# From the first projection to attention in a decoder trunk: finishing the projection's sums one by one, and another order of modulation rows and scores

## The chip, the core and the metric

The kernel runs on one core of a Trainium2 chip, in float32 from end to end. The metric is the device time in microseconds (us) of one execution, as the median of several runs. A profile is a recording of one further execution. PE is TensorE's matmul, PEld its weight load, DVE is VectorE, ACT ScalarE, POOL GpSimd and SP SyncE, which here only issues transfers (DMA).

## What is computed

The reference is one layer of a conditioned decoder, with a sequence of 512 tokens, a model width of 1024 and a feed-forward width of 2816. Cut to what matters, with the names of the code:

```python
mod = silu(c) @ w_ada + b_ada                       # six modulation rows of 1024
shift1, scale1, gate1, shift2, scale2, gate2 = split(mod, 6)

h = rmsnorm(x, norm1_g) * (1 + scale1) + shift1
qa, ka, va, qd, kd, vd, ga, gd = split(h @ w_in)    # 512,128,128,512,512,512,1024,1024 columns
out_a = sliding_window_attention(qa, ka, va)        # 8 query heads, 2 key/value heads of 64,
                                                    # window 128, ALiBi, a sink for each head
out_d = diff_attention(qd, kd, vd, lam)             # 4 heads, softmax1 - lam * softmax2, causal,
                                                    # ALiBi, RMS norm of each head
merged = sigmoid(ga) * (out_a @ w_branch_swa) + sigmoid(gd) * (out_d @ w_branch_diff)
x = x + gate1 * (merged @ w_out)
h2 = rmsnorm(x, norm2_g) * (1 + scale2) + shift2
x = x + gate2 * conv_ffn(h2)                        # up, causal convolution of width 3, GELU * gate, down
return rmsnorm(x, final_g)
```

The four modulation rows `gate1` to `gate2` are needed only behind the attention stage; `shift1` and `scale1` are needed at the very start.

## The kernel before

**Arithmetic.** Each float32 operand of a matmul is split into a high part, rounded to the matmul's number format (`f32r`), and a low part, the rest. A product is three matmuls: high by high, high by low, low by high (`mm3`). ACT writes the high part and DVE the low part (`split` for weights, `evac` for results that are read out of PSUM). Activations lie transposed, with channels on the partitions.

**PSUM.** Its eight banks (128 x 512 float32 each) are given out by tags: two of `f` (projections), three of `s` (scores), two of `t` (transposes) and one of `v` (attention values). A tile that takes a bank waits until the last reader of the bank's previous tile is through.

**Raw weights.** All weights and also the pieces of `w_ada` land in tiles of the tag `raw`, of which there are four. A transfer into such a tile is issued by SP once the tile's former contents have been read.

**The start.** Two modulation vectors, the norm of x and its transposes are made, and the first projection goes along with them: columns 0 to 767 of `w_in`, which are four blocks of 128 columns of q (two heads each), one of k and one of v. Its six sums, `acc6`, lie in six banks: `a0` and `a1` in the `f` banks, `a2` to `a4` in the `s` banks, `a5` in the `v` bank. There are eight groups, one for each 128 rows of `w_in`, and in each group `mm_k` does 18 matmuls in three parts (high by high, low weights, low h), each part over all six sums. In this stage the order on DVE, ACT and PE is that of the text.

**Reading the sums.** `evac` then reads q blocks 0 to 3 (L430), k (L432) and v (a copy `vaT`, L434); v is turned by four PE transposes into the bank `pva` (L436 to L438) and read from it into `va` (L441), which POOL has zeroed (L435). One transpose of small convolution weights (`pcv`, L445) comes next in the text.

**The attention stage.** From here to the stage's end the order on PE is that of the text, and that on ACT, DVE and POOL is decided by a scheduler, which puts first what is marked with `high_priority`: the work of scores, softmax and transposes with an offset `HP`, the modulation rows with half of it. PE's order is a weave of two kinds of work:

- Attention steps. `swa_scores(i, n0)` does the scores of a pair of heads (i of 4) for two blocks of queries; DVE adds the mask and takes maxima (L547). `swa_softmax(i)` has DVE compute the shifts (`nm`, L558), ACT the exponentials and DVE the sums and the scaling (L570). `swa_transpose(i, j)` turns the probabilities into the banks `tp` (L582), two banks for each head, which `evac` reads into `pTh` and `pTl`. `swa_values(i)` multiplies by v. The difference attention has the same four steps, `diff_scores`, `diff_softmax` (L670 to L685, tiles `sd`, `dmx`, `dls`), `diff_transpose` (L693) and `diff_values`, over s = 0 to 15, that is four heads by four blocks of queries.
- Projection units, queued by `add_head(h)` (q, k and v of head h of the difference attention, into `pq`, `pk` and so on) and `add_gate_a(j)` (the gate and the branch projection of 128 columns). `fill(n)` gives n ticks of them, and a tick is one `mm3` of 128 x 512. The numbers of ticks between attention steps are `SWA_FILL` and `DIFF_FILL`:

```python
    fill(SWA_FILL[0])
    swa_scores(0, 0)
    fill(SWA_FILL[1])
    swa_scores(0, 2)
    swa_softmax(0)
    fill(SWA_FILL[2])
```

After this the loop over the four pairs interleaves scores and softmax of pair i + 1 with transposes and values of pair i, and behind the loop come the units that are left and the loop over s.

**Modulation rows.** `ada_rows` computes the four later rows in halves of 512 columns. Each step loads 256 rows of `w_ada` (`ra`, L741) and adds two products on DVE (`arow`, L746 and L748); four steps make a half row. `fill` calls one step at every tick that is divisible by `ADA_EVERY` (8), from tick `ADA_START` (4) on. Behind the fourth step of a half row the sums are split, and one tick later `ada_spread` adds them over the partitions with two matmuls (`pr`, L757 and L758), copies them (L760) and has POOL write them to `mod_rows` in DRAM (L761), from where they are read behind the attention stage.

**The rest.** The gates of the difference branch, the merge, `w_out`, the feed-forward part (most of its matmuls are in L1112) and the last norm are the same in both kernels.

Of the kernel before, what the change touches and what calls it, by code (L numbers as in the profile page):

```python
# [8 lines left out]
F32 = mybir.dt.float32  # L9
# [5 lines left out]
P = 128  # L15
D = 1024
S = 512
KT = D // P
NT = S // P
# [9 lines left out]
ST = 6  # L29
ADA_LAG = 1  # L30
ADA_EVERY = 8
ADA_START = 4
V_LAG = 13
STAT_LAG = 10
NORM_LAG = 16
SWA_FILL = (4, 2, 3, 2, 2, 2, 2, 3)
DIFF_FILL = (3, 2, 4, 2)
WARM = 14
GROUPS = ((0,), (1,), (2,), (3,), (4,), (5,), (6,), (7,))
# [13 lines left out]
def kernel(  # L53
# [22 lines left out]
    nc = tc.nc  # L76
# [15 lines left out]
    def fbank(name):  # L92
        return bank("f", 2, [P, S], name)

    def sbank(name, shape=(P, S)):
        return bank("s", 3, list(shape), name)

    def tbank(name, shape=(P, S)):
        return bank("t", 2, list(shape), name)

    def vbank(name):
        return bank("v", 1, [P, S], name)
# [25 lines left out]
    ident = cpool.tile([P, P], F32, name="ident")  # L128
# [66 lines left out]
    hTh, hTl = parts_of("h"), parts_of("l")  # L195
# [28 lines left out]
    )  # L224
    nc.sync.dma_start(crow[0:66, :], conv_w[0].rearrange("t (a p) -> (t a) p", p=P))
    nc.sync.dma_start(crow[66:88, :], conv_b[0].rearrange("(a p) -> a p", p=P))
    acc6 = [fbank("a0"), fbank("a1"), sbank("a2"), sbank("a3"), sbank("a4"), vbank("a5")]
    man = ExitStack()
    man.enter_context(tc.manual_schedule(engines={nc.vector.engine, nc.scalar.engine, nc.tensor.engine}))
    cs = cpool.tile([P, 8], F32, name="cs")  # L230
# [91 lines left out]

    def mm_k(k, part):
        wh, wl = wts[k]
        lhs, rhs = ((wh, hTh), (wl, hTh), (wh, hTl))[part]
        for i in range(6):
            nc.tensor.matmul(
                acc6[i], lhs[:, i * P : (i + 1) * P], rhs[k],
                start=k == 0 and part == 0, stop=k == KT - 1 and part == 2,
            )  # L330


    def keep_warm(n):
# [88 lines left out]
    def evac(hi, lo, src, scale=None):  # L422
        if scale is None:
            nc.scalar.copy(hi, src)
            nc.vector.tensor_sub(lo, src, hi.bitcast(F32))
        else:
            nc.scalar.activation(hi, src, AF.Copy, scale=scale)
            nc.vector.scalar_tensor_tensor(lo, src, scale, hi.bitcast(F32), ALU.mult, ALU.subtract)

    for i in range(4):  # L430
        evac(qa[:, i, 0], qa[:, i, 1], acc6[i], qsc[:, i : i + 1])
    evac(ka[:, 0], ka[:, 1], acc6[4])  # L432
    vT = ap.tile([P, S], F32, tag="tmp", bufs=2, name="vaT")
    nc.scalar.copy(vT, acc6[5])  # L434
    nc.gpsimd.memset(va.bitcast(F32), 0.0)  # L435
    pv = tbank("pva")  # L436
    for t in range(NT):
        nc.tensor.transpose(pv[:, t * P : (t + 1) * P], vT[:, t * P : (t + 1) * P], ident)  # L438
    pv3 = pv.rearrange("p (t d) -> p t d", t=NT)
    for a, cc in ((0, 0), (64, 192)):  # L440
        evac(va[:, 0, :, cc : cc + 64], va[:, 1, :, cc : cc + 64], pv3[:, :, a : a + 64])  # L441


    pcv = tbank("pcv", (P, 88))
# [37 lines left out]
    def fill(n):  # L482
        for _ in range(n):
            if not current:
                prefetch()
                if loaded:
                    wts, run = loaded.pop(0)
                    current.append(run(wts))
                    prefetch()
            if current:  # L490
                try:
                    next(current[0])
                except StopIteration:
                    current.clear()
            for e in list(later):
                e[0] -= 1
                if e[0] <= 0:
                    later.remove(e)
                    e[1]()
            tick[0] += 1  # L500
            if tick[0] >= ADA_START and tick[0] % ADA_EVERY == 0:
                next(ada, None)
# [17 lines left out]
    def swa_scores(i, n0):  # L520
        if n0 == 0:
            c = pairs[i] = Pair()
            c.mx, c.nm, c.lsum, c.es = (
                ap.tile([P, 2, NT], F32, tag=t, bufs=2, name=f"{t}{i}") for t in ("mx", "nm", "lsum", "es")
            )
            c.sb = [ap.tile([P, 2, P], F32, tag="st0", bufs=2, name=f"st{i}_0")]
            c.sb += [ap.tile([P, 2, 256], F32, tag="st", bufs=ST, name=f"st{i}_{n}") for n in range(1, NT)]
            c.pT = []
        c = pairs[i]
        sps = [sbank(f"sw{i}_{n0}_{j}", (P, 2, 256)) for j in range(2)]  # L530
        for n in (n0, n0 + 1):
            w = P if n == 0 else 2 * P
            k0 = max(0, n - 1) * P
            qs, ks = slice(n * P, (n + 1) * P), slice(k0, k0 + w)
            mm3_rows([
                (
                    sps[j][:, n - n0, :w],
                    [qa[64 * j : 64 * j + 64, i, b, qs] for b in range(2)],
                    [ka[64 * j : 64 * j + 64, b, ks] for b in range(2)],
                )  # L540
                for j in range(2)
            ])
        for n in (n0, n0 + 1):
            w = P if n == 0 else 2 * P
            for j in range(2):
                with tc.high_priority(offset=HP):
                    nc.vector.tensor_tensor_reduce(  # L547
                        c.sb[n][:, j, :w], sps[j][:, n - n0, :w], dsw[:, 256 - w : 256], 1.0, -3e38, ALU.add, ALU.max,
                        c.mx[:, j, n : n + 1],
                    )  # L550
# [119 lines left out]
    def diff_softmax(s):  # L670
        with tc.high_priority(offset=HP):
            h, n = divmod(s, NT)
            slope = 2.0 ** (-2 * (h + 1))
            mx, pm = scored[s]
            lsum = ap.tile([P, 2], F32, tag="dls", bufs=3, name=f"dls{h}_{n}")
            nc.vector.tensor_scalar_mul(mx, mx, -slope)  # L676
            for m in range(2):
                nc.scalar.activation(  # L678
                    pm[m], pm[m], AF.Exp, bias=mx[:, m : m + 1], scale=slope, accum_out=lsum[:, m : m + 1]
                )  # L680
            nc.vector.reciprocal(lsum, lsum)
            nc.vector.tensor_mul(lsum[:, 1:2], lsum[:, 1:2], nlam)
            nc.vector.tensor_scalar_mul(pm[1], pm[1], lsum[:, 1:2])
            nc.vector.scalar_tensor_tensor(pm[0], pm[0], lsum[:, 0:1], pm[1], ALU.mult, ALU.add)
            probs[s] = pm[0]  # L685
# [112 lines left out]
    fill(SWA_FILL[1])  # L798
    swa_scores(0, 2)
    swa_softmax(0)  # L800
    fill(SWA_FILL[2])
    for i in range(SWA_PAIRS):
        more = i + 1 < SWA_PAIRS
        if more:
            swa_scores(i + 1, 0)
        fill(SWA_FILL[3])
        swa_transpose(i, 0)
        fill(SWA_FILL[4])
        swa_transpose(i, 1)
        if more:  # L810
            swa_scores(i + 1, 2)
        fill(SWA_FILL[5])
        if more:
            swa_softmax(i + 1)
        fill(SWA_FILL[6])
        swa_values(i)
        fill(SWA_FILL[7])
# [4 lines left out]
    ta = big.tile([P, KT, S], F32, tag="qa", name="ta")  # L822
    for j in range(2):
        add_gate_a(j)
    diff_scores(0, 1)
    diff_softmax(0)
    diff_softmax(1)
    fill(DIFF_FILL[0])
    for s in range(4 * DIFF_HEADS):
        h, n = divmod(s, NT)  # L830
# [412 lines left out]
    last = range(KT - TAIL, KT)  # L1243
# [482 lines left out]
```

## Time and profile before

| what | value |
|---|---|
| three runs, us | 719.83, 719.99, 721.53 |
| median, us | 719.99 |
| profiled execution, us | 722.67, with a span of 720.9 |
| mean granted clock of TensorE | 0.988 of full speed |
| PE busy | 693.5 us (96% of the span) |
| PEld busy | 604.8 us (84%) |
| DVE busy | 589.0 us (82%) |
| ACT busy | 381.5 us (53%) |
| POOL busy | 84.7 us (12%) |
| HBM read, written | 121.85 MB, 2.11 MB |

The span goes from the first to the last recorded instruction; the profiled execution's own time is 1.8 us longer than its span. A row of the instruction view gives the start (us from the span's start), the busy time of the row's instructions together, the engine, line, operation, output and inputs, the shape and the count; in brackets stand the idle time ahead of it and what ended that. The parts that the change touches lie between 57 and 160 us of the span.

### The profile page before, as it was taken

The numbers are of one execution on the slowest core, as the hardware profiler recorded it, in microseconds if no ns is written. First come the engines' busy times: TensorE is split into PE (matmuls) and PEld (weight loads), VectorE is DVE, ScalarE is ACT, GpSimd is POOL, SyncE is SP. The second block draws the span as 40 slices with busy tenths as digits, with TensorE's granted clock in tenths as the row PEclk, the third lists the DMA queues.
The fourth block names the chain that finished last, engine by engine and source line by source line (L and its number), as shares of the span: only waits on it lengthen the run. The fifth ranks groups of instructions, "written<-read, shape, count | busy, mean of one in ns | idle before, by whom it ended". The sixth has DMA issues, their size and how long they took to land. (4 is left out here: it accounts for less than half of the span.)

```text
span 720.9 us, 11252 instructions
## 1 busy us (share of the span) xinstructions
PE 693.5 (96%) x4172; PEld 604.8 (84%) x4172; DVE 589.0 (82%) x1121; ACT 381.5 (53%) x673; POOL 84.7 (12%) x101
## 2 busy tenths in 40 slices
PE   5998899999999999999999999999999999999994
PEld 5776788877887888888889999999999999778883
DVE  5998777887986674875379899888888999889996
ACT  3644656454554233432358666555656666555662
POOL 4000000000100110000012021111111212640000
PEclk8999999999999999999999999999999999999998
DMA  9886222534634565726827698877879769998502
GB/s 303 287 265 195 71 59 61 175 101 133 176 109 155 181 196 179 234 88 210 248 68 147 152 198 206 200 175 212 198 202 217 162 174 253 206 206 220 181 0 118
DMA packets 117367, 124.70 MB, mean 173 GB/s; under 512 B 4511, under 2 KB 93376, under 8 KB 117312
## 3 DMA queue, kind: packets, MB, share of 16 engines
q1 hardware_dynamic: 98254, 97.71, 42.8%
q0 software_dynamic: 18720, 25.73, 20.9%
q8 instruction: 33, 0.54, 0.3%
q10 hardware_dynamic: 338, 0.54, 0.2%
q14 instruction: 22, 0.18, 0.1%
HBM read 121.85 MB, written 2.11 MB: 172 GB/s over the span
## 5 line engine op out<-in xcount | busy, mean ns | idle before, releaser
L1112 PE MATMUL up<-t,m_whi 128*128 128x256 f32 x528 | 96.1, 283 | 0.0
L1112 PEld LDWEIGHTS up<-t,m_whi 128*128 128x128 f32 x528 | 82.4, 192 | 0.0
L1112 PE MATMUL up<-t,m_wlo 128*128 128x256 f32 x264 | 74.7, 283 | 0.1
L1112 PE MATMUL up<-bh,p_wlo 128*128 128x256 f32 x232 | 65.7, 284 | 0.6 <-DVE p_wlo L1055 0.6
L1112 PE MATMUL up<-bh,p_whi 128*128 128x256 f32 x232 | 65.6, 283 | 0.0
L1112 PE MATMUL up<-bl,p_whi 128*128 128x256 f32 x232 | 65.6, 283 | 0.0
L1112 PEld LDWEIGHTS up<-t,m_wlo 128*128 128x128 f32 x264 | 50.6, 192 | 0.3 <-DVE m_wlo L1055 0.3
L1112 PEld LDWEIGHTS up<-bh,p_wlo 128*128 128x128 f32 x232 | 44.4, 192 | 1.1 <-DVE p_wlo L1055 1.1
L748 DVE SCALAR_TENSOR_TENSOR arow<-ra,cs,arow 128x512 f32<-128x512 f32 x56 | 41.9, 748 | 3.9 <-DMA ra<-in_w_ada_dram 3.3
L1112 PEld LDWEIGHTS up<-bh,p_whi 128*128 128x128 f32 x232 | 44.5, 192 | 0.0
L1112 PEld LDWEIGHTS up<-bl,p_whi 128*128 128x128 f32 x232 | 44.5, 192 | 0.0
L1023 POOL DMA_DIRECT2D s<-in_w_up_dram x21 | 27.2, 1385 | 143.2 <-DMA s<-in_w_up_dram 60.1
L1055 DVE TENSOR_TENSOR m_wlo<-s,m_whi 128x1024 fp32r<-128x1024 f32 x31 | 37.8, 1219 | 2.0 <-ACT m_whi L1051 2.0
L1051 ACT CAST m_whi<-s 128x1024 fp32r<-128x1024 f32 x31 | 32.4, 1047 | 9.4 <-DVE s L1045 6.0
L174 POOL TENSOR_TENSOR r<-ms,mhalf 128x1 f32<-128x1 f32 (+1 forms) x16 | 13.5, 844 | 172.9 <-DVE ms L172 106.0
L1112 PE MATMUL up<-t,p_whi 128*128 128x256 f32 x176 | 32.2, 283 | 0.0
L678 ACT ACTIVATE sd<-sd,dmx 128x128 f32<-128x128 f32 (+3 forms) x32 | 17.8, 556 | 22.1 <-DVE dmx L676 15.6
L761 POOL DMA_DIRECT2D mod_rows<-arow x8 | 4.3, 540 | 205.4 <-ACT arow L760 205.2
L1112 PEld LDWEIGHTS up<-t,p_whi 128*128 128x128 f32 x176 | 27.4, 192 | 0.2 <-issue 0.2
L1119 ACT ACTIVATE gT<-a,cv 128x512 f32<-128x512 f32 x22 | 17.7, 814 | 17.7 <-DVE a L1154 17.3
L1051 ACT CAST p_whi<-wa 128x1024 fp32r<-128x1024 f32 x18 | 18.7, 1041 | 12.1 <-PE up L1112 9.0
L1112 PE MATMUL up<-t,p_wlo 128*128 128x256 f32 x88 | 24.9, 283 | 0.0
(476 smaller groups left out, 2125.3 us busy)
## 6 DMA issues: line engine op xcount, KB each, us to landing
ra<-in_w_ada_dram SPq DMA_DIRECT2D x32, 512.0 KB, 4.2
wa<-in_w_up_dram SPq DMA_DIRECT2D x22, 512.0 KB, 4.3
s<-in_w_up_dram SPq DMA_DIRECT2D x21, 512.0 KB, 4.8
s<-in_w_up_dram POOLq DMA_DIRECT2D x21, 512.0 KB, 6.5
adaw<-in_w_ada_dram SPq DMA_DIRECT2D x16, 512.0 KB, 5.1
w<-in_w_in_dram SPq DMA_DIRECT2D x12, 512.0 KB, 4.6
a<-in_w_up_dram SPq DMA_DIRECT2D x11, 512.0 KB, 4.7
b<-in_w_down_dram SPq DMA_DIRECT2D x10, 512.0 KB, 4.3
```

The source lines that it names most:

```text
L174: nc.gpsimd.tensor_tensor(r0, ms, mhalf[:, :n], ALU.pow)
L678: nc.scalar.activation(pm[m], pm[m], AF.Exp, bias=mx[:, m : m + 1], scale=slope, accum_out=lsum[:, m : m + 1])
L748: nc.vector.scalar_tensor_tensor(ac, r[:, a], cc, ac, ALU.mult, ALU.add)
L761: nc.gpsimd.dma_start(mod_rows[idx : idx + 1, hf * S : (hf + 1) * S], row)
L1023: nc.gpsimd.dma_start(dst, upblock(*blk), accum_op=ALU.add)
L1051: nc.scalar.copy(W[J, name][0], R[J, SRC[name]])
L1055: nc.vector.tensor_sub(lo, R[J, SRC[name]], hi.bitcast(F32))
L1112: nc.tensor.matmul(o[u], w[:, k, cu], b[:, k], start=name in ("p1", "m5", "p2") and k == 0 and x == 0, stop=k == 3 and x == 2, skip_group_ ...
L1119: nc.scalar.activation(grow(j), av[J][:, u], AF.Identity, bias=cv[:, 66 + j : 67 + j], scale=cv[:, 44 + j : 45 + j])
```

## The change

Four things change, all between the first projection's last group and the first blocks of the difference attention:

- **The order of the sums.** The six sums are taken in the order `DONE` = 0, 4, 2, 5, 1, 3 (q0, k, q2, v, q1, q3), in the giving out of banks and in all matmuls. In the last group the two low parts of a sum follow one another, so the sums are finished one by one and not all in the last part. The sums are read in the order q0, k, q2, v, q1, q3.
- **The turn of v.** The four transposes of v and their reading stand in `turn_va`, which is called one tick after the first softmax.
- **Modulation rows and fills.** `ADA_START` goes from 4 to 12, so the first step runs at tick 16 and not at tick 8, and all steps are one multiple of 8 ticks later. The first three fills go from 4, 2, 3 to 2, 1, 6 (nine ticks in both).
- **Difference scores.** `diff_scores` and `diff_softmax` of the first two blocks move from behind the pair loop into its last turn, where the scores and the softmax of a next pair would stand.

```diff
@@ -29,11 +29,11 @@
 ST = 6
 ADA_LAG = 1
 ADA_EVERY = 8
-ADA_START = 4
+ADA_START = 12
 V_LAG = 13
 STAT_LAG = 10
 NORM_LAG = 16
-SWA_FILL = (4, 2, 3, 2, 2, 2, 2, 3)
+SWA_FILL = (2, 1, 6, 2, 2, 2, 2, 3)
 DIFF_FILL = (3, 2, 4, 2)
 WARM = 14
 GROUPS = ((0,), (1,), (2,), (3,), (4,), (5,), (6,), (7,))
@@ -224,7 +224,9 @@
     )
     nc.sync.dma_start(crow[0:66, :], conv_w[0].rearrange("t (a p) -> (t a) p", p=P))
     nc.sync.dma_start(crow[66:88, :], conv_b[0].rearrange("(a p) -> a p", p=P))
-    acc6 = [fbank("a0"), fbank("a1"), sbank("a2"), sbank("a3"), sbank("a4"), vbank("a5")]
+
+    DONE = (0, 4, 2, 5, 1, 3)
+    acc6 = {i: (fbank, sbank, vbank)[(0, 0, 1, 1, 1, 2)[i]](f"a{i}") for i in DONE}
     man = ExitStack()
     man.enter_context(tc.manual_schedule(engines={nc.vector.engine, nc.scalar.engine, nc.tensor.engine}))
     cs = cpool.tile([P, 8], F32, name="cs")
@@ -322,12 +324,15 @@
 
     def mm_k(k, part):
         wh, wl = wts[k]
-        lhs, rhs = ((wh, hTh), (wl, hTh), (wh, hTl))[part]
-        for i in range(6):
-            nc.tensor.matmul(
-                acc6[i], lhs[:, i * P : (i + 1) * P], rhs[k],
-                start=k == 0 and part == 0, stop=k == KT - 1 and part == 2,
-            )
+        last = k == KT - 1
+        if last and part == 2:
+            return
+        for i in DONE:
+            for p in (1, 2) if last and part else (part,):
+                lhs, rhs = ((wh, hTh), (wl, hTh), (wh, hTl))[p]
+                nc.tensor.matmul(
+                    acc6[i], lhs[:, i * P : (i + 1) * P], rhs[k], start=k == 0 and p == 0, stop=last and p == 2
+                )
 
 
     def keep_warm(n):
@@ -427,18 +432,26 @@
             nc.scalar.activation(hi, src, AF.Copy, scale=scale)
             nc.vector.scalar_tensor_tensor(lo, src, scale, hi.bitcast(F32), ALU.mult, ALU.subtract)
 
-    for i in range(4):
+    nc.gpsimd.memset(va.bitcast(F32), 0.0)
+
+    def evac_q(i):
         evac(qa[:, i, 0], qa[:, i, 1], acc6[i], qsc[:, i : i + 1])
+
+    evac_q(0)
     evac(ka[:, 0], ka[:, 1], acc6[4])
+    evac_q(2)
     vT = ap.tile([P, S], F32, tag="tmp", bufs=2, name="vaT")
     nc.scalar.copy(vT, acc6[5])
-    nc.gpsimd.memset(va.bitcast(F32), 0.0)
-    pv = tbank("pva")
-    for t in range(NT):
-        nc.tensor.transpose(pv[:, t * P : (t + 1) * P], vT[:, t * P : (t + 1) * P], ident)
-    pv3 = pv.rearrange("p (t d) -> p t d", t=NT)
-    for a, cc in ((0, 0), (64, 192)):
-        evac(va[:, 0, :, cc : cc + 64], va[:, 1, :, cc : cc + 64], pv3[:, :, a : a + 64])
+    evac_q(1)
+    evac_q(3)
+
+    def turn_va():
+        pv = tbank("pva")
+        for t in range(NT):
+            nc.tensor.transpose(pv[:, t * P : (t + 1) * P], vT[:, t * P : (t + 1) * P], ident)
+        pv3 = pv.rearrange("p (t d) -> p t d", t=NT)
+        for a, cc in ((0, 0), (64, 192)):
+            evac(va[:, 0, :, cc : cc + 64], va[:, 1, :, cc : cc + 64], pv3[:, :, a : a + 64])
 
 
     pcv = tbank("pcv", (P, 88))
@@ -798,20 +811,29 @@
     fill(SWA_FILL[1])
     swa_scores(0, 2)
     swa_softmax(0)
-    fill(SWA_FILL[2])
+    fill(1)
+    turn_va()
+    fill(SWA_FILL[2] - 1)
     for i in range(SWA_PAIRS):
         more = i + 1 < SWA_PAIRS
         if more:
             swa_scores(i + 1, 0)
+        else:
+            diff_scores(0)
         fill(SWA_FILL[3])
         swa_transpose(i, 0)
         fill(SWA_FILL[4])
         swa_transpose(i, 1)
         if more:
             swa_scores(i + 1, 2)
+        else:
+            diff_scores(1)
+            diff_softmax(0)
         fill(SWA_FILL[5])
         if more:
             swa_softmax(i + 1)
+        else:
+            diff_softmax(1)
         fill(SWA_FILL[6])
         swa_values(i)
         fill(SWA_FILL[7])
@@ -822,9 +844,6 @@
     ta = big.tile([P, KT, S], F32, tag="qa", name="ta")
     for j in range(2):
         add_gate_a(j)
-    diff_scores(0, 1)
-    diff_softmax(0)
-    diff_softmax(1)
     fill(DIFF_FILL[0])
     for s in range(4 * DIFF_HEADS):
         h, n = divmod(s, NT)
```

## The prediction

> **What bounds the kernel now.** I read the page first, then the granted clock and busy time in short windows, then the instructions of PE, DVE and SP from 57 to 100 us and from 118 to 160 us, the two places that the change touches.
>
> ```profile
> span 720.9 us, 11252 instructions
> PE 693.5 (96%) x4172; PEld 604.8 (84%) x4172; DVE 589.0 (82%) x1121; ACT 381.5 (53%) x673; POOL 84.7 (12%) x101
> 65.29:68.70 3.41, 1.53 (x13) 1.00 (x12) 3.41 (x7) 0.00 (x0) 0.00 (x0) 1.00 0.45 151
> 68.70:72.11 3.41, 3.41 (x14) 2.23 (x12) 2.53 (x12) 0.37 (x1) 0.00 (x0) 0.50 0.72 205
> 85.76:120.00 34.24, 34.24 (x231) 28.95 (x230) 25.10 (x93) 23.26 (x73) 0.00 (x0) 1.00 0.17 48
> 150.00:160.00 10.00, 8.88 (x54) 6.99 (x52) 9.87 (x31) 4.53 (x12) 0.25 (x1) 1.00 0.50 150
> ```
>
> The window rows give PE, PEld, DVE, ACT and POOL busy, the granted clock, the DMA share and GB/s. PE is busy 96% of the span: time can come only from PE's waits and from its clock. Just after the first projection DVE is full while PE works 1.53 of 3.41 us, and in the next 3.41 us the clock is halved. From 85.76 to 120 PE never stops, so what is won before it is kept unless a later wait takes it back. The waits themselves, on PE:
>
> ```profile
> 59.88 1.56 PE L327 MATMUL a<-hTlB,w0h 128*128 128x512 f32 x6
> 61.90 0.50 PE L118 MATMUL pq<-hThA,w_h 128*128 128x512 f32 x1 [0.46 <-DVE qa L428]
> 66.11 0.32 PE L125 MATMUL sw<-ka,qa 64*128 64x128 f32 x1 [0.61 <-DVE qa L428]
> 67.43 0.32 PE L125 MATMUL sw<-ka,qa 64*128 64x128 f32 x1 [1.00 <-DVE qa L428]
> 78.58 1.13 PE L582 MATMUL tp<-ident,st 128*128 128x128 f32 x7 [0.97 <-DVE st L570]
> 82.31 1.01 PE L582 MATMUL tp<-ident,st 128*128 128x128 f32 x7 [1.20 <-DVE pTl L425]
> 96.55 0.93 PE L582 MATMUL tp<-ident,st 128*128 128x128 f32 x7
> 157.97 0.30 PE L693 MATMUL td<-ident,sd 128*128 128x128 f32 x1 [1.12 <-DVE sd L684]
> ```
>
> Every releaser is DVE. These are its rows there, with the products of the modulation rows (arow) in 60 to 69 us as one group (DVE's busy time comes first), and the landing time of their loads:
>
> ```profile
> 61.10 0.75 DVE L428 SCALAR_TENSOR_TENSOR qa<-a,qsc,qa 128x512 fp32r<-128x512 f32 x1
> 64.64 0.75 DVE L748 SCALAR_TENSOR_TENSOR arow<-ra,cs,arow 128x512 f32<-128x512 f32 x1 [1.48 <-DMA ra<-in_w_ada_dram]
> 67.30 0.68 DVE L425 TENSOR_TENSOR ka<-a,ka 128x512 fp32r<-128x512 f32 x1
> 60.00:69.00 9.00, 3.58 (x6) 0.00 (x0) 0.00 (x0) 0.98 0.78 250
> DMA to landing us min/median/max: 3.7/4.2/5.1
> 59.55 0.37 SPq L741 DMA_DIRECT2D ra<-in_w_ada_dram  x1
> ```
>
> Between the low parts of the four q sums and of k (61.10 to 67.30) DVE does products and waits 1.48 us for a load issued at 59.55. The scores need k, so they wait for all of it.
>
> **Part 1, sums one by one, products later, other fills.** The number of matmuls is unchanged. In the last group the first sum's last matmul is the eighth of 18 instead of the thirteenth: five places of 1.56/6.7 = 0.23 us earlier. ACT reads it at about 59.2, DVE at 60.0. With k second in line and no product ahead, DVE has q0, k and q2 done at 60.0 + 0.66 + 0.6 + 0.66 = 61.9. The bank that pq waits for is free at 60.7, before PE's last sum, so its 0.46 us goes. The transpose for cv (0.24 us) moves ahead of the last group; that and the memset of va, on an idle POOL, cost nothing.
>
> The built order of the changed kernel shows what comes instead. DVE's queue becomes: q1 and q3 between two products of load 1, the split of v's weights, four score maxima, a product of load 2, and only then the other four maxima and the softmax; then the second product, the scaling, a product of load 3, and the reading of the first transposes. Load 2 uses load 1's slot and load 3 load 2's, so each is issued when DVE has done both products of the one before. A DMA latency thus stands in DVE's queue, with PE's scores and transposes behind it. On SP the loads move behind the next head's weights, which aren't needed before 95 us.
>
> I walk that queue with row durations (pitches: product 0.66, 512-wide low part 0.6 to 0.66, split 1.14, wide maximum 0.34; a duration in a row contains about 0.1 of overlap).
>
> ```profile
> 74.28 0.36 DVE L558 TENSOR_SCALAR nm<-mx,nsink 128x4 f32<-128x4 f32 x2
> 88.93 1.08 DVE L570 TENSOR_SCALAR st<-st,lsum 128x128 f32<-128x128 f32 x4
> 92.58 1.22 DVE L115 TENSOR_TENSOR w_l<-w,w_h 128x1024 fp32r<-128x1024 f32 x1
> 83.62 1.16 DVE L425 TENSOR_TENSOR pTl<-tp,pTh 128x512 fp32r<-128x512 f32 x2 [0.30 <-ACT pTh L424]
> 72.89 0.42 DVE L547 CUSTOM_DVE_ANT_0 st<-sw,dsw 128x256 f32<-128x256 f32 x1 [1.66 <-PE sw L125]
> ```
>
> Load 1 lands at 57.7 + 4.2 = 61.9, in time. Product, q1, product: 63.7, and load 2 goes out. q3, split, four maxima: 66.6. Load 2, with less traffic, takes 3.9 (between minimum and median) and lands at 67.65. Product, four maxima, nm: 69.95. Second product: 70.6; load 3 (alone: 3.7) lands at 74.4, while exponentials and the first scaling end at 73.6. Product to 75.05; then sums, va, second scaling (0.98) and three maxima, 2.75 us: 77.8. The first reading of transposes takes 0.6, and PE's second transposes start at 78.4 instead of 82.31: 3.9 earlier.
>
> DVE then has a backlog. Reading, product, q, reading, maxima, nm: 82.9. Load 4, issued at 79.5, lands at 83.2. From there two products 1.3, two splits 2.3, sums 0.4, two scalings 1.95 with 0.35 between, three 512-wide reads 1.8, four maxima 1.1: 9.25 us to 92.5, and 0.6 for the reading that frees the bank of PE's next second transposes: 93.1. PE could be there at 96.55 - 3.9 = 92.65. They start at 93.15: **3.4 us earlier** than before. After it DVE has no product until the last pair's values, so this stands. The ends: with every load at the 5.1 maximum the same walk gives 97.85, a loss of 1.3; with no load wait at all the gain is bounded by the waits in the PE rows and half of the slow clock window, 0.46 + 0.61 + 1.00 + 0.97 + 1.20 + 1.7 = 5.9. I take 3.4, since DMA is idle around loads 3 and 4.
>
> **Part 2, scores of the difference attention inside the last pair.**
>
> ```profile
> 122.25 0.68 DVE L425 TENSOR_TENSOR qkv<-pk,qkv 128x512 fp32r<-128x512 f32 x1
> 124.02 1.16 DVE L425 TENSOR_TENSOR pTl<-tp,pTh 128x512 fp32r<-128x512 f32 x2 [1.09 <-ACT pTh L424]
> 124.86 0.93 PE L582 MATMUL tp<-ident,st 128*128 128x128 f32 x7
> 134.02 0.41 ACT L678 ACTIVATE sd<-sd,dmx 128x128 f32<-128x128 f32 x1 [3.45 <-DVE dmx L676]
> 134.94 0.17 DVE L681 RECIPROCAL dls<-dls 128x2 f32<-128x2 f32 x1 [0.22 <-ACT sd L678]
> 135.65 0.35 DVE L684 SCALAR_TENSOR_TENSOR sd<-sd,dls,sd 128x128 f32<-128x128 f32 x1
> ```
>
> Before, PE meets no wait here: the last transposes start at 124.86, and the fills after them cover the softmax. Afterwards DVE's order puts the whole softmax of block 0 between the k read (ends 122.85) and pTl. Two maxima and a multiply: 123.4. ACT's two exponentials, ahead of its copy pTh, from 123.55 to 124.35. Reciprocal to last product, 134.94 to 135.92 in the rows: 125.35. First half of pTl 0.6: 126.0. PE arrives at 125.0 (two matmuls moved away, 0.46 less, six score matmuls more), waits 1.05, and 0.2 again for the second half. With 0.15 for a second short block of scores that is **1.4 lost**. Ends: 0, if ACT and DVE run ahead of PE by that much; 2.0, if the weights of the gate (split 0.6 before PE needs them) also come late.
>
> **Part 3, the wait at 157.97.** It stands behind four products:
>
> ```profile
> 150.00:158.00 8.00, 2.71 (x4) 0.00 (x0) 0.25 (x1) 1.00 0.43 130
> ```
>
> The new order has none there (these rows come later by 8 steps); a split of 1.14 and a read of 0.6 take part of their place. With both chains moved on by part 2 I get the result at 158.35 against PE at 158.25: of 1.12 about 0.25 stays, **0.85 won** (ends 0 and 1.1).
>
> The last modulation row comes 8 steps, some 6 us, later:
>
> ```profile
> 307.49 0.48 POOL L761 DMA_DIRECT2D mod_rows<-arow  x1 [21.72 <-ACT arow L760]
> 335.91 1.37 POOL L1023 DMA_DIRECT2D s_t<-in_w_up_dram  x1 [27.94 <-DVE c L936]
> ```
>
> POOL has 27.94 us free behind it: no cost. If that cover were gone it would cost those 6 us.
>
> **The sum.** -3.4 + 1.4 - 0.85 = -2.85. The profiled execution took 722.67 us at a span of 720.9, so 719.8; the median of the three runs is 719.99, which these waits belong to as well: 717.1. Ends for this case, from landing times of 3.7 to 4.2 us each and part 2 between 1.0 and 1.6: 715.9 to 718.4. 0.3% of the time, 2.2 us, is about what a measurement of this kernel can tell from no change; the threshold is at 717.8.
>
> **Rivals.**
> 1. The loads land late. For: 1.48 waited at 64.64 for a load of 5.1. Against: that was with DMA share 0.98 to 1, and the loads now go out when it is low. At 5.1 us each part 1 is +1.3: 719.99 + 1.3 + 1.4 - 0.85 = 721.8, slower. Part 1 falls by 4.7 for 1.2 us of mean landing time, so the sum is zero at 3.9 + 2.85/3.9 = 4.6 us.
> 2. The clock halves on the critical path. For: the first two window rows: a window with PE busy 1.53 of 3.41 and no wait over 1.00 us was followed by 3.41 us at 0.50. In the walk PE has nothing from 76.2 to 78.4, 2.2 us, more than the 1.88 idle there. Half speed for 3.41 us loses 1.7, less the 0.5 that PE waits for DVE anyway: 718.3. Against: the wait may fall across two such windows, and an earlier halving would be hidden in it. The Trainium skill (TensorE: Matmul & The Clock Gate, "HAM oscillation — how this bites in real kernels") asks only that no idle gap exceed some 3.4 us; by that this rival has no chance and the time stays 717.1. The trace disagrees: gaps of at most 1.00 us sufficed, so the rival keeps its chance.
> 3. Part 2 is free, because DVE reaches it ahead of PE: 717.1 - 1.4 = 715.7. Against: the k read and the copy of the pair's values come from PE itself.
> 4. It doesn't do what it says: DVE, full in both places, only trades one queue for another: 720.0.
>
> **Chances.** Forecast 0.50 (three quarters of it under 717.8), late loads 0.16, clock 0.13, free part 2 0.13, nothing won 0.08. Faster by over 0.3%: 0.38 + 0.13 + 0.01 = 0.52. Slower by over 0.3% needs late loads together with the clock or the 2.0 end: 0.10. Within: 0.38. The range leaves out a tenth on each side: 715.2 to 721.2.
>
> **What would show it.** Right: pq without a wait near 61.3; DVE waiting for ra loads before the second maxima (about 1 us) and before the product after the first scaling (about 0.8); second transposes near 78.4 and 93; a new wait of about 1 us on pTl in the last pair; the wait at 157.97 mostly gone. Wrong: no DVE wait on a load (part 1 nearer 5), waits of 2 us and more (rival 1), 0.50 clock after 78 us (rival 2), no wait in the last pair (rival 3).

## The result and the profile after

The changed kernel takes **730.19 us** (median of four runs, 729.82 to 730.97) beside 719.91 for the kernel before (four runs, 718.76 to 721.53): a ratio of **1.0134, 95% interval 1.0113 to 1.0155**. It is slower by 10.3 us, where 2.9 faster was forecast.

The head of the page after:

```profile
span 729.2 us, 11250 instructions
PE 695.7 (95%) x4172; PEld 605.5 (83%) x4172; DVE 588.6 (81%) x1121; ACT 381.2 (52%) x673; POOL 84.8 (12%) x101
```

PE is busy 2.2 us longer than before (695.7 against 693.5) and idle 6.1 us longer (33.5 against 27.4), so most of the loss is waiting. The changed kernel's lines have other numbers: L697 is the old L684 (the last product of a difference softmax), L761 the old L748 (a product for the modulation rows), L430 the old L425. PE's instructions after that carry the steps of the prediction (start, busy time, operation, and in brackets the idle time ahead and its releaser):

```profile
60.41 0.40 PE L118 MATMUL pq<-hThA,w_h 128*128 128x512 f32 x1
66.10 1.65 PE L125 MATMUL sw<-ka,qa 64*128 64x256 f32 x11 [1.52 <-DVE mx L560]
79.27 0.93 PE L595 MATMUL tp<-ident,st 128*128 128x128 f32 x7
93.83 1.01 PE L595 MATMUL tp<-ident,st 128*128 128x128 f32 x7 [0.22 <-DVE pTl L430]
123.58 1.01 PE L595 MATMUL tp<-ident,st 128*128 128x128 f32 x7 [1.00 <-DVE pTl L430]
153.08 0.63 PE L706 MATMUL td<-ident,sd 128*128 128x128 f32 x4 [0.99 <-DVE sd L697]
159.38 0.30 PE L706 MATMUL td<-ident,sd 128*128 128x128 f32 x1 [1.07 <-DVE sd L697]
204.13 0.63 PE L706 MATMUL td<-ident,sd 128*128 128x128 f32 x4 [0.78 <-DVE sd L697]
230.17 0.63 PE L706 MATMUL td<-ident,sd 128*128 128x128 f32 x4 [2.14 <-DVE sd L697]
314.63 0.50 PE L118 MATMUL pB<-outdA,wbd 128*128 128x512 f32 x1 [1.62 <-ACT wbd L114]
317.01 0.50 PE L120 MATMUL pB<-outdA,wbd 128*128 128x512 f32 x1 [1.64 <-DVE wbd L115]
341.32 0.50 PE L1187 MATMUL oc<-wo_h,mg0h 128*128 128x512 f32 x1 [0.68 <-DVE c L951]
```

Up to 94 us the second transposes of pairs 0 and 1 start earlier than before (79.27 and 93.83 against 82.31 and 96.55), and the one wait of the last pair, pair 3, is there. What the prediction did not have begins at 153: waits on `sd`, the softmax in the blocks of the difference attention, on `wbd`, weights of the difference branch, at 315, and on `c` at 341, the reading of a bank that the next sum (`oc`) takes over.

To see where the time goes, the table follows the same PE instruction in both kernels. The last matmul group that both have ahead of the first projection's last group is the reduction `pa`, before and then after:

```profile
55.17 0.58 PE L264 MATMUL pa<-ones,ac 128*128 128x1 f32 x4
54.21 0.58 PE L266 MATMUL pa<-ones,ac 128*128 128x1 f32 x4
```

The kernel after stands 0.96 us earlier there already. In that stretch the change alters only the order of the sums, and the 0.96 belongs to these executions: the profile before has two windows of 3.41 us at half the clock there (14.09 to 20.91), the one after has one (14.53 to 17.95), and two runs below have it the other way round: run 4, with the changed kernel's code up to there, has two and reaches `pa` at 55.07, and run 2, with the code of the kernel before, has one and reaches it at 53.69. So all differences are counted from this group on (start after - start before + 0.96; minus is a lead). The pairs are counted from 0, the difference blocks (four to a head) too.

| up to | lead or lag, us | gained or lost on the way |
|---|---|---|
| second transposes of pair 2, 110.8 us | -1.69 | -1.69 |
| second transposes of pair 3, 124.86 | -0.32 | +1.37 |
| difference block 4, 157.97 | +2.37 | +2.69 |
| block 7, 177.90 | +1.35 | -1.02 |
| block 15, 226.52 | +4.61 | +3.26 |
| first `oc`, 331.88 | +8.30 | +3.69 |
| end of the span | +9.26 | +0.96 |

The front gains, the last pair costs, and then 9.6 us are lost between 125 us and the end. Not all of a row is waiting, because some of PE's work stands on the other side of a mark in the changed kernel. PE's idle time in the table's rows from that of pair 3 on is, before and after, 0 and 1.00, 1.12 and 2.73, 0.37 and 0, 0.33 and 2.92, 0.46 and 3.50, 12.70 and 13.45 us.

### The profile page after: what moved, and what is told of

It is laid out like the page before. It is cut to its first block, busy times and chain, and to the rows that moved or that the text cites. A ratio compares the mean times of both kernels' runs of the same rounds, so it can differ in the third digit from the quotient of the medians.

```text
span 729.2 us, 11250 instructions
## 1 busy us (share of the span) xinstructions
PE 695.7 (95%) x4172; PEld 605.5 (83%) x4172; DVE 588.6 (81%) x1121; ACT 381.2 (52%) x673; POOL 84.8 (12%) x101
## 5 line engine op out<-in xcount | busy, mean ns | idle before, releaser
L761 DVE SCALAR_TENSOR_TENSOR arow<-ra,cs,arow 128x512 f32<-128x512 f32 x56 | 41.9, 749 | 3.8 <-DMA ra<-in_w_ada_dram 2.7
L1131 PEld LDWEIGHTS up<-t,p_whi 128*128 128x128 f32 x176 | 27.4, 192 | 0.2 <-issue 0.2
```

Of the source, the lines that this page charges most:

```text
L761: nc.vector.scalar_tensor_tensor(ac, r[:, a], cc, ac, ALU.mult, ALU.add)
L1131: nc.tensor.matmul(o[u], w[:, k, cu], b[:, k], start=name in ("p1", "m5", "p2") and k == 0 and x == 0, stop=k == 3 and x == 2, skip_group_ ...
```

## The experiments

All compare with runs of the kernel before on the same chip; each ratio is to that kernel, with its 95% interval. "Lead" and "lag" are counted as in the table, each from the run's own `pa`.

### Which edit costs it

**1. First step back at tick 8**, the rest of the change kept:

```diff
-ADA_START = 12
+ADA_START = 4
```

> Theory A (the steps' new place): starting the modulation-row steps 8 ticks later puts their products, their loads and their sums beside other work from 140 us on; in the changed kernel that costs 9.6 us between 137 us (1.0 ahead of the kernel before) and the end (8.3 behind). With the first step back at tick 8 everything from 140 us on is as in the kernel before, and the time is 719 to 722.5, according to what of the front's 2.7 us goes with it. Rival B (the difference scores' new place): they cost it, and the time stays at 728 to 731.

Measured: 720.28 us, ratio 0.9998 (0.9983 to 1.0013). All of the loss is gone.

**2. The kernel before with `ADA_START = 12`** and nothing else:

> The kernel before with the first step at tick 16 and nothing else changed. Theory A: slower, 724 to 730, with waits of PE on L684 (sd) of 2 us near 228 and waits on wbd near 310. Rival B: 717 to 720.

Measured: 731.91 us, 1.0146 (1.0125 to 1.0166), 1.9 us above the range of theory A. One number, 4 to 12, makes the slowdown alone. PE waits 2.14 us on `sd` at 229 and 1.64 on `wbd` at 316, as in the changed kernel, and 2.24 on `sd` at 138, which the changed kernel doesn't. At each of these three places the clock is at one half for 3.41 us in this profile, which it isn't in the changed kernel's.

**3. The difference scores behind the loop again**, the late steps kept:

> The changed kernel with the two difference scores and softmaxes behind the pair loop again. Theory A: only the wait of 1.0 on pTl in the last pair goes and perhaps that on sd near 153: 726.5 to 730. Rival B: 717 to 721.

Measured: 728.66 us, 1.0120 (1.0087 to 1.0153). Theory A holds, rival B falls. The wait on `pTl` in the last pair is gone, and PE waits 2.23 us on `sd` at 136 instead.

**4. Two steps at tick 48**, which from there on puts the steps where they were before:

```diff
 next(ada, None)
+if tick[0] == 48:
+    next(ada, None)
```

> The changed kernel with two steps at tick 48, so that the steps start 8 ticks later but are from tick 48 on where they were in the kernel before. Theory A: the front keeps its 2.7 us and the rest is as before: 717 to 721. Rival B: 728 to 731.

Measured: 723.66 us, 1.0036 (1.0019 to 1.0054). It comes 2.7 us above the range of theory A. The double step has its price: PE waits 2.89 us on `sd` at 159.83. But from block 4 on (lag 1.96) to the end (1.30) nothing more is lost.

### Where and by what

**5. ACT's copy of the finished row first:**

```diff
-nc.scalar.copy(row, pr[0:1, :])
+with tc.high_priority(offset=HP):
+    nc.scalar.copy(row, pr[0:1, :])
```

> The changed kernel with ACT's copy of a finished half row (L773) given the same precedence as the softmax; nothing is left out. In the changed kernel that copy of the seventh half row starts 3.3 us behind its matmuls, its write lands 4.8 us after that, the products of the eighth wait for it until 301.7 and hold two of the four raw tiles, and SP can issue the next gate's weights only at 303.0. Theory M2 (held raw tiles): the waits of PE on wbd, 1.62 and 1.64 us, shrink by 2 us or more, and the time is 726.5 to 728.5. Rival (the loads are late by themselves): 729.5 to 731.

Measured: 732.32 us, 1.0164 (1.0140 to 1.0188), above both ranges. The copy started 1.1 us behind the end of its matmuls and not 2.7, but the write still took 5 us to land and the eighth half row began at 300.67, by the time from `pa` no earlier than the 301.66 of the changed kernel. The copy's place was not what mattered, so this run says nothing for or against the held tiles.

**6 and 7. Two steps at tick 104, or at tick 184** (the edit of run 4 with another number):

> The changed kernel with two steps at tick 104 (near 170 us): later than before up to there, as before behind it. If the waits on sd from 200 to 230 us (3.4 us of loss beside the kernel with steps at tick 8) and those on wbd and c from 309 to 341 (4.4) both come from the steps' place, 721.5 to 724. If only the first stretch to 160 us counted and the rest followed from it, 729 to 731.

> The same with two steps at tick 184 (near 250 us). If both places cost by themselves, it keeps the waits of 0.8 and 2.1 on sd near 204 and 230 and loses those on wbd: 725 to 727.5, some 3.4 above the kernel that catches up at tick 104. If only one of them counts, it equals that kernel or the changed one (730).

Measured: 725.13 us, 1.0063 (1.0043 to 1.0084), and 725.82, 1.0078 (1.0054 to 1.0102). The first is 1.1 us above its range, the second in it, but 0.7 above the first and not 3.4. By their times the two can't be told apart, since the double step at tick 104 costs something itself (waits of 0.63, 0.89 and 0.93 at 173 to 180 us). The traces separate the places. From block 7 to block 15 the first loses 0.16 us and the second 3.26; from block 15 to the first `oc` they lose 0.00 and 0.07, where the changed kernel lost 3.69. So the two places cost by themselves, and what comes after 250 us depends on where the last half row is done.

**8. The products on POOL:**

```diff
-nc.vector.scalar_tensor_tensor(ac, r[:, a], cc, ac, ALU.mult, ALU.add)
+nc.gpsimd.tensor_mul(r[:, a], r[:, a], cc.to_broadcast([P, S]))
+nc.gpsimd.tensor_add(ac, ac, r[:, a])
```

(The first product of a half row, a multiplication alone, goes to POOL in the same way.)

> The changed kernel with the modulation products on POOL, as a multiplication and an addition each, and none on DVE (64 products, 44 us of DVE's busy time). Theory M1 (the products stand ahead of the softmax in DVE's queue): the waits on sd at 153, 159, 204 and 230 us and the 1.5 at 66 go, 717 to 725, according to whether the last half row is still late. Rival: DVE's order isn't the cause, but the loads in the raw tiles, or POOL takes over 3 us for a product and makes them later still: 729 or more.

Measured: 787.86 us, 1.0937 (1.0909 to 1.0965). That is where the rival had it, but it doesn't decide about DVE's queue: PE's waits on `sd` stay (6.9 us between 60 and 400 us) though no product is left on DVE, while POOL takes long for a product, DVE's own rows get slower beside it, and `wbd` comes later still (10.3 us of waits). The groups of POOL:

```profile
L761 POOL TENSOR_TENSOR arow<-arow,ra 128x512 f32<-128x512 f32 x56 | 77.3, 1381 | 3.3
L759 POOL TENSOR_TENSOR ra<-ra,cs 128x512 f32<-128x512 f32 x56 | 62.5, 1133 | 87.0 <-DMA ra<-in_w_ada_dram 32.8 <-DVE mx L560 26.8 <-DVE pTl L430 10.5
```

A product takes 2.5 us there (1133 and 1381 ns), where DVE's one instruction takes 0.75. Beside it DVE's scaling of 256 columns (L583) went from 349 to 436 ns and its subtraction of 128x1024 weights in SBUF (`wgd_l`, L115) from 1223 to 1654, while `pTl` (L430), which reads PSUM, stayed at 687 and 685. The Trainium skill (GPSIMD Engine Reference, "8. Key points") says that POOL shares its SBUF interfaces with VectorE, with contention for DVE instructions in a 2-port mode or with two SBUF inputs, and that DVE is about twice as fast elementwise. This trace agrees for the subtraction, which has two SBUF inputs, and for the speed of a single instruction (1381 ns for a sum, against 688 for DVE's subtraction of 512 columns); in which mode the scaling ran, no run shows. The price of a product is more than three times DVE's, because DVE needs one instruction for two.

**9. The finished row copied into another tile**, so that the next half row waits for no write:

```diff
-row = ac[0:1, :]
+row = ah[0:1, :]
...
-nc.gpsimd.dma_start(mod_rows[idx : idx + 1, hf * S : (hf + 1) * S], row)
+nc.gpsimd.dma_start(mod_rows[idx : idx + 1, hf * S : (hf + 1) * S], row.bitcast(F32))
```

> The changed kernel with the finished row copied into the tile of the sums' high part and written to DRAM from there, so that the next half row's first product waits for no write (the rows are rounded to the matmul's format by this; the work is the same). If the write of the seventh half row (4.8 us from issue to landing) is what holds the raw tiles and so the weights wgd and wbd, the waits on wbd near 315 us and on c near 341 are mostly gone: 725 to 727.5. Rival (these weights come late because SP asks for them later and the queue is full): 729.5 to 731.

Measured: 728.37 us, 1.0117 (1.0092 to 1.0142). The waits on `wbd` and on `c` are gone, as expected. The time is 0.9 us above the range, and its interval overlaps that of the changed kernel, so no gain is shown. Other waits have come: 1.46, 1.48 and 1.09 us on `pTl` at 93, 109 and 125 us (from pair 0 to pair 3 this kernel loses 5.07 us, the changed one 1.76), and from 130 to 345 us these are the largest:

```profile
PE td L706 <- DVE sd L697: 3.2, 4, 1.4
PE pga L118 <- ACT ta L783: 1.7, 1, 1.7
PE od L119 <- DVE aTl L430: 1.6, 1, 1.6
```

(total, times, longest). The products now start earlier, as no write holds them, and meet other work; that this makes the new waits is argued and not shown. What held `wbd` is shown by this run; that it can be had for nothing is not.

**10. Products of 8 columns** in place of 512 (all but the first of each half row), with all loads left:

```diff
-nc.vector.scalar_tensor_tensor(ac, r[:, a], cc, ac, ALU.mult, ALU.add)
+nc.vector.scalar_tensor_tensor(ac[:, :8], r[:, a, :8], cc, ac[:, :8], ALU.mult, ALU.add)
```

> The changed kernel with 56 of the 64 products done on 8 of their 512 columns (the modulation rows are left incomplete); loads, raw tiles and waits stay. If DVE's time for the products is what makes the softmax late, the waits on sd at 153, 159, 204 and 230 us shrink by 3.5 us or more in sum, and the time is 720 to 725. If it is what DVE waits for in its queue (a load, a weight's high part), they stay, and the time is 728 or more.

Measured: 724.05 us, 1.0059 (1.0037 to 1.0081). The same list of waits, first after, then in this run:

```profile
PE td L706 <- DVE sd L697: 5.4, 5, 2.1
...
PE td L706 <- DVE sd L697: 2.2, 3, 1.1
```

The waits on `sd` shrink by 3.2 us, a little less than the 3.5 asked for. Between the last pair and block 15 this kernel loses 1.02 us, the changed one 4.93. DVE's time for the products makes most of that loss. The loads keep their order on SP, but go out earlier by the clock (the last at 294.95 and not 304.54), and the waits on `wbd` are gone too, so not all of the 6.1 us between the two kernels' times is won in the blocks.

### What stays without the late steps

**11. Steps and difference scores as before**, so that the sums' order, the turn of v and the fills remain:

> The changed kernel with the first step at tick 8 and the difference scores behind the loop: what stays of the change is the order of the sums, the turn of v and the fills. The profile of the kernel with steps at tick 8 is 2.2 us ahead at 111 us and loses 1.1 in the last pair; without that loss 717.5 to 719.5. If the front's lead is given back further on, 719.5 to 721.

Measured: 720.00 us, 0.9996 (0.9982 to 1.0010). The profiled execution took 717.88 and shows no loss in the last pair; the twelve runs spread from 717.33 to 720.82.

**12. The kernel before with the sums' order alone** (`DONE`, the last group's matmuls, the order of reading; the turn of v, fills, steps and scores stay):

> The kernel before with only the order of the sums, their finishing one by one and their reading changed. By the first part of the prediction the waits for the bank of pq (0.46) and for k (1.89 before the scores) go and a later one comes: 718 to 719.6. If DVE's queue is what sets the scores' time anyway: 719.6 to 721.

Measured: **717.76 us, 0.9964 (0.9952 to 0.9977)**. This version is faster than both kernels.

### Late, or at the wrong place

The last four start from run 12 and move the steps only: to ticks 4, 12, 20 and so on; to ticks 12, 20 and so on; to ticks 24, 32 and so on; to every seventh tick.

```diff
-if tick[0] >= ADA_START and tick[0] % ADA_EVERY == 0:
+if tick[0] >= ADA_START and tick[0] % ADA_EVERY == 4:   # ADA_START 4, and 12
```

```diff
-ADA_START = 4
+ADA_START = 20
```

```diff
-ADA_EVERY = 8
+ADA_EVERY = 7
```

> The sums' order alone, with the steps 4 ticks earlier (ticks 4, 12, 20 and so on). Theory L (lateness): at most 1 us from the base's 717.8, 717 to 718.8. Theory P (phase against the blocks): the products meet other softmaxes, 719.5 to 724.

> The sums' order alone, with the steps 4 ticks later (ticks 12, 20 and so on). Theory L: part of the cost of 8 ticks, 720 to 724, growing evenly from 157 us to the end. Theory P: anything from 717 to 730, with the loss at single blocks.

> The sums' order alone, with the first step at tick 24, 16 later. Theory L: more than the 10.7 us of 8 ticks, 732 to 742, since the last half row's sums come some 12 us later than in the kernel before, beside the last weights of the merge. Theory P: less than that of 8 ticks, 719 to 728.

> The sums' order alone, with a step every 7 ticks from tick 7 on. The last half row is done 32 ticks (some 22 us) earlier. Theory L: no wait on wbd or c, and no loss, 716.5 to 718.5. Theory P: the products meet all blocks in turn, waits of PE on sd of 1 us or more in several places, 720 to 726.

| steps | us | ratio to the kernel before |
|---|---|---|
| 4 ticks earlier | 721.69 | 1.0027 (1.0008 to 1.0046) |
| as before (run 12) | 717.76 | 0.9964 (0.9952 to 0.9977) |
| 4 later | 722.72 | 1.0037 (1.0022 to 1.0052) |
| 16 later | 730.14 | 1.0135 (1.0108 to 1.0161) |
| every 7 | 728.26 | 1.0118 (1.0095 to 1.0140) |

Earlier costs too: 4 ticks earlier lose 2.3 us between blocks 7 and 11 and 3.9 between block 15 and the first `oc`, there with a wait of 1.98 on `ta` at 256 and a window of 3.41 us at half the clock behind it. 4 later loses at a single block (PE waits 4.17 us on `sd` at 224.73) and not evenly; 16 later costs 1.7% beside its base, hardly more than 8 later beside its own (1.5%, run 2); and steps every 7 ticks, whose last half row is done early, lose 10 us beside run 12. That speaks for theory P, the steps' place against the blocks, though two of its ranges were too low (the last two runs) and the wait on `ta` is not one of a block's softmax. In the run with every 7 (run 16), PE waits at the fourth block of each head:

```profile
150.83 0.94 PE L702 MATMUL td<-ident,sd 128*128 128x128 f32 x4 [2.08 <-DVE sd L693]
178.76 0.63 PE L702 MATMUL td<-ident,sd 128*128 128x128 f32 x4 [2.21 <-DVE sd L693]
206.70 0.63 PE L702 MATMUL td<-ident,sd 128*128 128x128 f32 x4 [2.19 <-DVE sd L693]
233.61 0.63 PE L702 MATMUL td<-ident,sd 128*128 128x128 f32 x4 [2.16 <-DVE sd L693]
```

The heads follow one another by 27 to 28 us, and so do the half rows on DVE, whose first products run, for two of these heads, at

```profile
172.69 0.48 DVE L755 TENSOR_SCALAR arow<-ra,cs 128x512 f32<-128x512 f32 x1
200.69 0.48 DVE L755 TENSOR_SCALAR arow<-ra,cs 128x512 f32<-128x512 f32 x1
```

so the same collision comes back in every head. Theory L keeps one place: the wait on `wbd` is absent 4 ticks earlier, 4 later and at every 7, and there with 8 and 16 later (1.64 and 1.52 us).

## Why the prediction was wrong

**The step that failed** stands at the end of its third part: "The last modulation row comes 8 steps, some 6 us, later" (8 ticks are meant), judged to cost nothing because POOL has 27.94 us free behind it. That looks at the row's last consumer alone. The steps are 32, each with a load, two products and a raw tile, and all of them move by 8 ticks, not the last only. The prediction walked the queues in the two places that the diff touches in the text, 57 to 100 and 118 to 160 us, and took the rest as unchanged. In its place the runs show that the later steps alone cost 1.46% (run 2) and that nothing of the loss is left without them (run 1). 6.95 us were lost between 178 and 332, 5.6 of them as more idle time of PE.

**Blocks of the difference attention (+2.69 - 1.02 + 3.26).** DVE's rows at block 15, first after, then before:

```profile
224.65 2.33 DVE L761 SCALAR_TENSOR_TENSOR arow<-ra,cs,arow 128x512 f32<-128x512 f32 x3
...
228.13 1.23 DVE L115 TENSOR_TENSOR wba_l<-wba,wba_h 128x1024 fp32r<-128x1024 f32 x1
229.27 0.75 DVE L697 SCALAR_TENSOR_TENSOR sd<-sd,dls,sd 128x512 f32<-128x512 f32 x1
```

```profile
210.45 2.33 DVE L748 SCALAR_TENSOR_TENSOR arow<-ra,cs,arow 128x512 f32<-128x512 f32 x3
...
225.62 0.75 DVE L684 SCALAR_TENSOR_TENSOR sd<-sd,dls,sd 128x512 f32<-128x512 f32 x1
```

Three products of load and sum that before ran at 210, while PE had other work, now stand at 224.65 between the maxima and the softmax of the widest block; `sd` is ready 3.65 us later than before by the clock of the profile, and PE waits 2.14. The split of `wba` has come ahead of the softmax's last product, too. Run 10 took the products' time away and most of the loss with it.

**The last half row (+3.69).** The rows after, in order:

```profile
295.93 0.57 ACT L773 COPY arow<-pr 1x512 f32<-1x512 f32 x1
296.79 0.49 POOL L774 DMA_DIRECT2D mod_rows<-arow  x1 [20.23 <-DVE wbd L115]
301.66 0.49 DVE L759 TENSOR_SCALAR arow<-ra,cs 128x512 f32<-128x512 f32 x1 [4.56 <-issue]
302.96 0.37 SPq L477 DMA_DIRECT2D wgd<-in_w_in_dram  x1
306.85 1.05 ACT L114 CAST wgd_h<-wgd 128x1024 fp32r<-128x1024 f32 x1 [9.46 <-DMA wgd<-in_w_in_dram]
311.59 1.05 ACT L114 CAST wgd_h<-wgd 128x1024 fp32r<-128x1024 f32 x1 [3.17 <-DMA wgd<-in_w_in_dram]
313.54 1.04 ACT L114 CAST wbd<-wbd 128x1024 fp32r<-128x1024 f32 x1
...
DMA to landing us min/median/max: 1.6/2.7/4.8
```

The row of the seventh half leaves `arow` when its write has landed (the last line is of the writes of the eight rows). The profile names no releaser for DVE's row at 301.66, but 296.79 and the longest landing time, 4.8, make 301.6. Only then does DVE touch the loads of the eighth, which sit in raw tiles, and SP gets a tile for the next gate's weights (`wgd`) when the first of them is read. That load and the next one of `wgd` (out at 306.58) come late: ACT waits 9.46 us for the first and 3.17 for the second, and the cast of `wbd`, whose load went out at 296.53, stands behind them. Before, the same cast waited for PE only:

```profile
304.12 1.06 ACT L114 CAST wbd<-wbd 128x1024 fp32r<-128x1024 f32 x1 [1.40 <-PE pB L120]
```

Two runs remove this wait by different means (7 by an earlier half row, 9 by freeing `arow`). No rival of the prediction covers this: rival 1 has loads that take long to land, at the front only, and here a load goes out late because its tile is held.

**Part 1 (forecast -3.4, measured -2.08 and -1.76 at the second transposes of pairs 0 and 1).** The sums one by one do what was said: `pq` at 60.41 waits for nothing. Of DVE's waits for loads the first is there, ahead of the second maxima; the second, at the product after the first scaling (0.8 forecast), is not, and 0.45 comes at the load after that. Those three products:

```profile
67.44 0.75 DVE L761 SCALAR_TENSOR_TENSOR arow<-ra,cs,arow 128x512 f32<-128x512 f32 x1 [1.05 <-DMA ra<-in_w_ada_dram]
74.36 0.75 DVE L761 SCALAR_TENSOR_TENSOR arow<-ra,cs,arow 128x512 f32<-128x512 f32 x1
83.94 0.75 DVE L761 SCALAR_TENSOR_TENSOR arow<-ra,cs,arow 128x512 f32<-128x512 f32 x1 [0.45 <-DMA ra<-in_w_ada_dram]
```

What is missing is the clock. Its windows after (PE, PEld, DVE, ACT, POOL busy, the granted clock, DMA share, GB/s):

```profile
62.31:65.73 3.42, 1.82 (x14) 1.00 (x10) 3.42 (x9) 0.00 (x0) 0.00 (x0) 1.00 0.31 79
65.73:69.14 3.41, 3.04 (x15) 2.42 (x16) 2.36 (x10) 0.00 (x0) 0.00 (x0) 0.50 0.73 235
69.14:72.56 3.42, 3.42 (x12) 2.84 (x11) 1.78 (x8) 2.29 (x10) 0.00 (x0) 0.50 0.31 65
```

Two windows at half speed stand where before there was one, 6.46 us of work against 3.41, some 1.5 us more. PE then reaches the second transposes of pair 0 later than DVE is ready (at 79.27 it waits for nothing), those of pair 1 not quite (0.22 at 93.83). What the second window costs can be read from other executions, because runs 4, 6 and 7 have the changed kernel's code up to ticks 48, 104 and 184. Run 4 has two such windows between 60 and 80 us and leads by 1.94 and 1.71 us at the two places; run 7 has one and leads by 3.50 and 3.02; run 6 has none and leads by 3.52 and 3.02. So the second window costs some 1.3 us at pair 1, it comes in some executions of the same code and not in others, and without it part 1 falls short by 0.4. This is rival 2, earlier than it was placed, and beside part 1 rather than in its place. Run 12 has no halved window there and leads by 3.25 us at the second transposes of pair 1:

```profile
63.00:68.00 5.00, 4.58 (x34) 3.15 (x33) 4.99 (x14) 0.00 (x0) 0.00 (x0) 1.00 0.62 209
68.00:73.00 5.00, 4.85 (x28) 3.41 (x27) 4.86 (x20) 3.84 (x13) 0.00 (x0) 1.00 0.36 116
```

**Part 2 (forecast +1.4)** held in kind: the wait on `pTl` is 1.00, and 1.37 are lost between pairs 2 and 3, of which 0.37 is PE's own work, moved. With the steps at tick 8 (run 1) the loss there is 1.12, of which only 0.28 is that wait, and with the scores moved back as well (run 11) there is none. Whether it costs time at the end is not shown: the medians of runs 1 and 11 differ by 0.28 us.

**Part 3 (forecast -0.85)** fell: the wait is 1.07, as long as before (1.12). No product stands ahead of it any more, as the prediction said, but the two rows that it let take a part of their place are long enough:

```profile
156.30 1.22 DVE L115 TENSOR_TENSOR w_l<-w,w_h 128x1024 fp32r<-128x1024 f32 x1
157.44 0.68 DVE L430 TENSOR_TENSOR aTl<-td,aTh 128x512 fp32r<-128x512 f32 x1
```

With the steps at tick 8, and so with products ahead of it, runs 1, 11 and 12 have it at 1.06 to 1.14 too, so the wait doesn't hang on the products alone.

**Open** is why run 11 doesn't keep the 2.2 us of run 12. Their profiles lead by 3.13 and 2.97 us at the end, but the medians differ, and the profile of run 11 is of one of its three fastest executions. The turn of v and the fills may bring the halved window back in others. The mean granted clock on record fits that in part, with 0.996 and 0.995 in the two fastest of run 11 (717.33 and 717.88 us), 0.990 to 0.994 in the other ten and 0.992 to 0.997 in run 12; but the third fastest (718.52) stands at 0.991, and no trace shows where the clock fell.

## What to carry to other kernels

A constant that shifts a periodic filler moves every one of its instances, so each place where an instance lands has to be walked, to the last one: its products in the busiest engine's queue and the buffers that its loads hold, not only its result's due time. Where the filler's period is near that of the main loop, a wrong phase comes back in every round, and a shift to earlier can cost as much as one to later (4 ticks either way: 0.6 and 0.7% beside run 12). A bundle of edits is worth taking apart: here one of them gains 0.36%, and another costs four times that.

## What was not expected of the hardware

A wait of PE can cost more than its length. In the run with the steps 4 ticks later PE waits 4.17 us for `sd`, and the clock is then at one half for two windows (columns as above):

```profile
220.17:223.58 3.41, 0.39 (x2) 0.00 (x0) 3.41 (x10) 1.91 (x3) 0.00 (x0) 1.00 0.65 202
223.58:227.00 3.42, 2.27 (x8) 1.89 (x8) 1.53 (x3) 0.59 (x1) 0.00 (x0) 0.50 0.86 264
227.00:230.41 3.41, 3.41 (x14) 3.00 (x12) 0.16 (x1) 0.00 (x0) 0.00 (x0) 0.50 0.01 3
```

PE's 5.68 us of work in them is worth 2.84 at full speed. In run 2 a window with 1.27 of 3.41 us busy was followed by one at half speed, and in the run with every 7 ticks one with 1.32 of 3.40; the longest waits there were 2.14 and 2.08 us. The Trainium skill (TensorE: Matmul & The Clock Gate, "HAM oscillation — how this bites in real kernels") puts the limit at a gap of some 3.4 us: the 4.17 us above agree with it, the two shorter ones don't. Nor is it certain: in the changed kernel the wait of 2.14 us at 230 was not followed by a halved window, and at the front the same code had none, one or two of them (runs 6, 7 and 4). A gain or a loss of some 1.5 us in one profile can be such a window, and not the edit.
